# Eight DRAM-to-DRAM copies of kept cache rows, moved from the first feed-forward layer to the prompt's attention

## The chip, the cores and the metric

The kernel runs on one core of a Trainium2 chip. The metric is the device time of one execution, in microseconds. Before the change it is 1665.25 us (median of 3 runs, 1664.86 to 1665.97). TensorE (PE) multiplies, VectorE (DVE), ScalarE (ACT) and GpSimd (POOL) do elementwise work, and SyncE (SP) issues nearly all DMA transfers. Each engine works through its own list of instructions in the order in which it was built.

## The reference, cut to what matters

A two-layer decoder step on a 512-token prompt and 8 sampled sequences of 8 tokens. Layer 0 mixes by pooling, layer 1 by sparse attention; each layer is followed by a gated feed-forward network (FFN) with a causal convolution of width 3. All is float32.

```python
def conv_ffn(x, prefix, w_up, conv_w, conv_b, w_down):
    up = x @ w_up                       # 1024 -> 2 * 2816
    up_pad = jnp.concatenate([prefix, up], 1)
    c = conv_b
    for k in range(CONV_W):
        c = c + conv_w[k] * up_pad[:, k:k + T]
    g, u = jnp.split(c, 2, -1)
    return (jax.nn.silu(g) * u) @ w_down, up_pad[:, -(CONV_W - 1):]

def nsa_sample(...):
    ...
    buf_len = win_buf.shape[1]          # 512
    wkv = jnp.concatenate([win_buf, win_kv], 1)
    ...
    return o @ w_o, cmp_kv, slc_kv, wkv[:, -buf_len:]
```

The last value is the output `win_kv_s`: for each of the 8 sequences the 512 rows of its window, 8 of them new. The other 504 rows are those of the input `state_win_kv`, shifted by 8. They take part in no computation on the way to this output: they are copied from one place in DRAM to another, 1008 KB for each sequence.

## The kernel before

The activations of all 576 tokens stand in SBUF with the channels on the partitions, split into a high and a low part (`xh`, `xl`), so that three matmuls on rounded numbers make one precise product. A weight is split in the same way: SP fetches it into a raw buffer (`rawa`, two of them; line 235), ACT copies it to the rounded high part (`wha`, line 257), and DVE subtracts to get the low part (`wla`, line 258). Three pairs of high and low buffers take turns, so a split waits until PE is done with the pair three before it.

The FFN goes through its 2816 inner channels in units of 256. The unit that begins at chunk m0 of 128 channels has two weight blocks (gate and up). PE computes eight products for it, each of 24 matmuls of 288 columns (tiles `u`, line 166): for j in 0, 1 (which 128 channels), for each half of the tokens, for q in 0, 1 (gate, up). ACT then copies each product to SBUF (lines 419 to 421), starts the convolution (line 426), DVE finishes it (lines 427 and 428), ACT takes the silu (line 453), and DVE multiplies (line 454). After every second unit come the products of the down projection for the four chunks before (tiles `d`), with two weight blocks of their own, 192 matmuls in all. So the sequence of PE's work around the middle of layer 0 is: up 8, up 10, down of 4 to 7, up 12, up 14, down of 8 to 11, up 16, up 18, and so on, each of 192 matmuls.

In the program `keep_window(b)` (line 380) issues one of the eight copies, from SP. In layer 0 it is called behind the loads of the units m0 = 2 to 16, one copy for each.

The order of instructions on each engine is not the order of the code: a scheduler sets it when the program is built, by durations that it assumes for instructions and transfers. Moving a transfer in the code can therefore also move the instructions of other engines.

The prompt's attention comes much later, after the sampled tokens' attention. It works on 16 items (query head r of a group, pair p of key groups, branch j), four items for each r. An item's scores (`psp`, line 1534) go into two double banks of PSUM by turns, and DVE drains them (line 1539) into `P`; ACT takes exponentials (line 1540), POOL scales (line 1553), PE transposes (`ppp`) and multiplies with the values (`pop`, line 1582). `queries(r)` (line 1459) loads the queries of r from DRAM into `qs` with four DMAs (line 1462), `queries2(r)` transposes them on PE (`pq`) and copies them to `Q`. There are two buffers `qs`, so the load for r waits until the transposes of r - 2 are done. `plan` (line 1598) says at which item each of these steps is emitted: for r = 2 at item 4, for r = 3 at item 8.

Of the kernel before, what the change touches and what calls it, by code (L numbers as in the profile page):

```python
# [21 lines left out]
NB = 8  # L22
# [107 lines left out]
def body(tc, top, I, O):  # L130
    nc = tc.nc
# [28 lines left out]
    def f32(ap):  # L160
        return ap.bitcast(F32)
# [34 lines left out]
    def mmt(name, group="any", n=1):  # L196
        p_, size = banks[group]
        return p_.tile([128, 512] if n == 1 else [128, n, 512], F32, tag="ps" + group, name=name, bufs=size)
# [3 lines left out]
    def transpose(out, in_):  # L202
        pe.transpose(out, in_, ident[:in_.shape[0], :in_.shape[0]])
# [3 lines left out]
    def evac(out, in_):  # L207
        evac_turn[0] ^= 1
        if evac_turn[0]:
            act.activation(out, in_, AF.Copy)  # L210
        else:
            dve.tensor_copy(out, in_)
# [167 lines left out]
    def keep_window(b):  # L380
        rows = "(p j) k g c -> p (j k g c)"
        sp.dma_start(O["win_kv_s"][0, b, 0:WIN - TS].rearrange(rows, j=4), I["state_win_kv"][0, b, TS:WIN].rearrange(rows, j=4))

    def ffn(l, U, ctx, opening, closing, first=None):
# [22 lines left out]
        def products(blk, j, hf, name):  # L407
            p_ = mmt(name)
            terms = [(wt[:, k, j * 128:(j + 1) * 128], xt[:, k, hf * HALF:(hf + 1) * HALF])
                     for k in range(KD) for wt, xt in ((blk[0], xh), (blk[0], xl), (blk[1], xh))]  # L410
            mm3(p_[:, :HALF], terms)
            return p_

        def conv(m, pa, pb):
            u = fp.tile([128, UW + 8], F32, tag="u", name=f"u{l}{m}", bufs=4)
            us = u[:, 2 + TP:UW].rearrange("p (b t) -> p b t", t=2 + TS)
            pool.memset(u[:, 0:2], 0.0)
            pool.tensor_copy(us[:, :, 0:2], sTv[:, :, m].rearrange("p (b k) -> p b k", k=2))
            act.activation(u[:, 2:2 + HALF], pa[:, :HALF], AF.Copy)
            act.activation(u[:, 2 + HALF:2 + TP], pb[:, :TP - HALF], AF.Copy)  # L420
            act.activation(us[:, :, 2:], pb[:, TP - HALF:HALF].rearrange("p (b t) -> p b t", t=TS), AF.Copy)  # L421
            pool.tensor_copy(col[:, :, m].rearrange("p (j i) -> p j i", i=2),  # L422
                             u[:, TP:TP + 90].rearrange("p (j i) -> p j i", i=10)[:, :, 0:2])
            cf = fp.tile([128, UW], F32, tag="c", name=f"c{l}{m}", bufs=4)
            c = cf[:, 0:CW]
            act.activation(c, u[:, 2:UW], AF.Identity, bias=cv[:, 132 + m:133 + m], scale=cv[:, 88 + m:89 + m])  # L426
            dve.scalar_tensor_tensor(c, u[:, 1:1 + CW], cv[:, 44 + m:45 + m], c, OP.mult, OP.add)  # L427
            dve.scalar_tensor_tensor(c, u[:, 0:CW], cv[:, m:m + 1], c, OP.mult, OP.add)
            return cf

        def up(chunks):
            for c0 in range(0, len(chunks), 2):
                m0 = chunks[c0]
                wv = I["ffn_w_up"][l].rearrange("(k p) n -> p k n", p=128)
                if m0 == 0 and first:
                    wg, wu = first
                else:
                    wg = U.load(wv[:, :, m0 * 128:(m0 + 2) * 128])
                    wu = U.load(wv[:, :, FF + m0 * 128:FF + (m0 + 2) * 128])
                if l == 0 and 2 <= m0 < 2 + 2 * NB:  # L440
                    keep_window(m0 // 2 - 1)
                order = [(j, hf, q) for hf in range(2) for j in range(2) for q in range(2)] if m0 == 0 else \
                        [(j, hf, q) for j in range(2) for hf in range(2) for q in range(2)]
                pr = {}
                for n, (j, hf, q) in enumerate(order):
                    pr[j, hf, q] = products((wg, wu)[q], j, hf, f"u{l}{m0}{j}{hf}{q}")
                    if m0 == 0:
                        opening(n)
                for j in range(2):
                    m = m0 + j  # L450
                    cg = conv(m, pr[j, 0, 0], pr[j, 1, 0])
                    cu = conv(NF + m, pr[j, 0, 1], pr[j, 1, 1])
                    act.activation(cg[:, 0:CW], cg[:, 0:CW], AF.Silu)
                    dve.tensor_tensor(cu[:, 0:CW], cg[:, 0:CW], cu[:, 0:CW], OP.mult)
                    hh = fp.tile([128, T], F32R, tag="hh", name=f"hh{l}{m}", bufs=8)
                    hl = fp.tile([128, T], F32R, tag="hl", name=f"hl{l}{m}", bufs=8)

                    def views(full):
                        return (full[:, 0:TP], full[:, TP:].rearrange("p (b t) -> p b t", t=TS))

                    cs = (cu[:, 0:TP], cu[:, 2 + TP:2 + TP + 80].rearrange("p (b t) -> p b t", t=10)[:, :, 0:TS])
                    for hv, lv, s in zip(views(hh), views(hl), cs):
                        act.activation(hv, s, AF.Copy)
                        dve.tensor_tensor(lv, s, f32(hv), OP.subtract)
                    hp[m] = (hh, hl)
# [22 lines left out]
        def down(chunks, first, last):  # L488
# [11 lines left out]
            for m, hf in ([(m, hf) for hf in range(2) for m in range(KD)] if last else [(m, hf) for m in range(KD) for hf in range(2)]):  # L500
# [10 lines left out]
                if last:  # L511
                    closing(hf, m)
                    if hf == 0 and m in (3, 5):
                        state_out(m // 4)

        up(list(range(0, 4)))
        for g in range(1, 5):
            up(list(range(4 * g, 4 * g + 4)))
            down(list(range(4 * g - 4, 4 * g)), g == 1, False)
        up([20, 21])  # L520
        down(list(range(16, 22)), False, True)

# [873 lines left out]
    def prompt_attention(ctx):  # L1396
# [62 lines left out]
        def queries(r):  # L1459
            qs = qp.tile([128, 4, 256], F32, tag="qs", name=f"qs{r}")  # L1460
            for t in range(4):
                sp.dma_start(qs[:, t].rearrange("p (g c) -> p g c", g=4),
                             qd[t * 128:(t + 1) * 128].rearrange("p (g r c) -> r p g c", g=4, r=4)[r])
            gate[r] = gpv[:, :, :, r]
            return qs

        def queries2(r, qs):
            Q[r] = pa.tile([128, 2, TP], F32, tag="QT", name=f"Q{r}")
            for p in range(2):
                pt = tpt(f"pq{r}{p}")  # L1470
                for t in range(4):
                    transpose(pt[:, t * 128:(t + 1) * 128], qs[:, t, p * 128:(p + 1) * 128])
                evac(Q[r][:, p], pt)

        def cmp_scores(r):
            pk = mmt(f"pk{r}")
            for g in range(4):
                pe.matmul(pk[32 * g:32 * g + 32], KB[:, g], Q[r][:, g // 2], start=True, stop=True, tile_position=(0, 32 * g))
            ks = pp.tile([128, TP], F32, tag="ks", name=f"ks{r}", bufs=1)
            act.activation(ks, pk, AF.Copy, scale=-1.0)  # L1480
            return ks
# [24 lines left out]
        def cmp_probs(r, ec):  # L1506
            pt = tpt(f"pct{r}")
            for t in range(4):
                transpose(pt[:, t * 128:(t + 1) * 128], ec[:, t].rearrange("p g n -> p (g n)"))
            cmpp[r] = ptp.tile([128, TP], F32, tag="pc", name=f"pc{r}")  # L1510
            evac(cmpp[r], pt)
# [81 lines left out]
        for t in range(4):  # L1593
            keys(t)
            if t == 0:
                queries2(0, q0)
        pend = {}
        plan = {0: lambda r: pend.update(q=queries(r)), 1: lambda r: queries2(r, pend["q"]), 2: lambda r: pend.update(k=cmp_scores(r)),
                3: lambda r: pend.update(e=cmp_softmax(r, pend["k"])), 4: lambda r: cmp_probs(r, pend["e"])}
        n = len(items)  # L1600
        for i in range(n + 3):
# [11 lines left out]
            for r in range(1, 4):  # L1613
                k = i - 4 * (r - 1)
# [83 lines left out]
    with ExitStack() as ck:  # L1698
        with ExitStack() as cl:
# [10 lines left out]
            def opening(i):  # L1710
                norm[i][1].run(tile_steps(0))
                return during_first_half(norm[i][1])
# [107 lines left out]
        with ExitStack() as c1:  # L1820
            prompt_attention(c1)
# [41 lines left out]
```

## Time and profile before

| what | value |
|---|---|
| median of 3 runs | 1665.25 us |
| the profiled execution's own time | 1669.55 us |
| its span, first to last instruction | 1667.7 us |
| mean granted TensorE clock | 0.978 |
| PE busy | 1588.7 us, 95% |
| DVE, ACT, POOL busy | 61%, 45%, 23% |
| the eight copies | issued by SP from 44.3 to 256.4 us, 1008 KB each |

A profiled execution is one run on the chip, with the start and end of each instruction. All rows below are from it, and its own time is some 4 us over the median. Times in the rows are microseconds from the start of the span. An instruction's idle time is how long its engine stood still just before it, and the releaser is the instruction that ended the wait.

### The profile page before, as it was taken

What the parts mean: (1) busy time and instruction counts of PE and PEld (TensorE: products, weight loads), DVE (VectorE), ACT (ScalarE), POOL (GpSimd) and SP (SyncE); (2) the same over time, 40 slices, a digit from 0 to 9 for tenths busy, and PEclk for the clock granted to TensorE, in tenths of its full rate; (3) what the DMA queues carried; (4) which work ended last, traced back from release to release, by engine and by line L of the source; (5) the groups of instructions that cost most, each with busy time, mean ns of one, the idle gap of its engine ahead of it and who ended that gap; (6) DMA issues with size and microseconds to landing.
All of it is one profiled execution on the core that took longest, in us unless ns stands there. A gap on an engine that the chain in (4) does not pass through costs nothing.

```text
span 1667.7 us, 32288 instructions
## 1 busy us (share of the span) xinstructions
PE 1588.7 (95%) x13207; PEld 1485.2 (89%) x13207; DVE 1013.6 (61%) x2053; ACT 758.5 (45%) x1406; POOL 391.1 (23%) x597
## 2 busy tenths in 40 slices
PE   7999979899999999999999988999999999999995
PEld 7999979899999999999996764556999999999995
DVE  7665344454557435898878967675465645454547
ACT  5655141434335332466565665655255534334332
POOL 3222000011102001343333316662122201111104
PEclk9999988999999999999999998999999999999997
DMA  5334223222224684664549960004212223232211
GB/s 194 110 129 149 76 75 126 77 83 70 102 65 171 211 235 130 185 242 159 179 166 377 415 165 4 1 1 129 84 33 95 77 77 102 77 101 77 78 60 57
DMA packets 122323, 206.06 MB, mean 124 GB/s; under 512 B 18543, under 2 KB 98505, under 8 KB 112592
## 3 DMA queue, kind: packets, MB, share of 16 engines
q1 hardware_dynamic: 112272, 134.49, 25.4%
q0 software_dynamic: 9216, 67.11, 10.8%
q10 hardware_dynamic: 688, 2.40, 0.5%
q8 instruction: 104, 1.70, 0.4%
q14 instruction: 43, 0.35, 0.1%
HBM read 187.10 MB, written 24.84 MB: 127 GB/s over the span
## 4 chain that ended last, share of the span: by engine, by line
PE 78%; DVE 9%; issue 4%; POOL 4%; ACT 3%; DMA 2%; SPq 0%; ACTq 0%; POOLq 0%; DVEq 0%
PE u L166 32%; PE d L166 14%; PE pr L921 11%; PE pj L166 7%; PE wo L166 2%; POOL P L1553 2%; PE psp L1534 2%; DVE wla L258 1%; PE pop L1582 1%; PE po L1336 1%; DVE kf L1213 1%; PE pj L716 1%; DMA sr<-in_cache_slc_kv,idx 1%; PE pss L1241 1%; ACT P L1540 1%
## 5 line engine op out<-in xcount | busy, mean ns | idle before, releaser
L166 PE MATMUL u<-xh,wha 128*128 128x288 f32 x704 | 210.5, 299 | 7.9 <-ACT wha L257 7.9
L166 PE MATMUL u<-xh,wla 128*128 128x288 f32 x704 | 210.4, 299 | 7.6 <-DVE wla L258 7.6
L166 PE MATMUL u<-xl,wha 128*128 128x288 f32 x704 | 210.7, 299 | 0.3 <-POOL xl L352 0.2
L166 PE MATMUL u<-xl,whb 128*128 128x288 f32 x704 | 208.0, 296 | 0.2
L166 PE MATMUL u<-xh,whb 128*128 128x288 f32 x704 | 207.3, 295 | 0.0
L166 PE MATMUL u<-xh,wlb 128*128 128x288 f32 x704 | 207.2, 295 | 0.0
L422 POOL COPY fcol<-u 128x18 f32<-128x18 f32 x88 | 62.8, 726 | 506.4 <-ACT u L421 506.4
L427 DVE SCALAR_TENSOR_TENSOR c<-u,convp,c 128x592 f32<-128x592 f32 x88 | 71.9, 831 | 160.6 <-ACT c L426 160.6
L166 PEld LDWEIGHTS u<-xh,wla 128*128 128x128 f32 x704 | 134.6, 191 | 8.8 <-DVE wla L258 8.8
L166 PEld LDWEIGHTS u<-xh,wha 128*128 128x128 f32 x704 | 134.7, 191 | 8.4 <-ACT wha L257 8.4
L258 DVE TENSOR_TENSOR wlb<-rawb,whb 128x2048 fp32r<-128x2048 f32 x37 | 84.8, 2292 | 87.8 <-ACT whb L257 87.8
L166 PEld LDWEIGHTS u<-xl,wha 128*128 128x128 f32 x704 | 134.7, 191 | 2.0 <-DVE xl L352 1.1
L166 PEld LDWEIGHTS u<-xl,whb 128*128 128x128 f32 x704 | 132.0, 188 | 1.9 <-DVE xl L352 1.1
L258 DVE TENSOR_TENSOR wla<-rawa,wha 128x2048 fp32r<-128x2048 f32 (+1 forms) x52 | 99.3, 1917 | 54.2 <-ACT wha L257 54.2
L166 PEld LDWEIGHTS u<-xh,whb 128*128 128x128 f32 x704 | 132.0, 188 | 0.1
L166 PEld LDWEIGHTS u<-xh,wlb 128*128 128x128 f32 x704 | 132.0, 188 | 0.0
L510 DVE SCALAR_TENSOR_TENSOR xz<-xz,d 128x288 f32<-128x288 f32 x160 | 70.4, 450 | 97.4 <-PE d L166 96.8
L257 ACT ACTIVATE whb<-rawb 128x2048 fp32r<-128x2048 f32 x37 | 70.8, 1914 | 115.2 <-DMA rawb<-in_ffn_w_up 32.3
L257 ACT ACTIVATE wha<-rawa 128x2048 fp32r<-128x2048 f32 (+1 forms) x52 | 82.8, 1611 | 71.4 <-PE d L166 39.5
L166 PE MATMUL d<-hh,wha 128*128 128x288 f32 x352 | 105.5, 301 | 4.1 <-ACT wha L257 4.0
L921 PE MATMUL pr<-xlo,W1h 128*128 128x256 f32 x512 | 103.9, 285 | 2.5 <-DVE xlo L896 2.5
L894 ACT ACTIVATE xhi<-xf 128x1024 fp32r<-128x1024 f32 (+1 forms) x68 | 70.1, 1031 | 77.6 <-PE pr L921 55.6
(662 smaller groups left out, 4532.6 us busy)
## 6 DMA issues: line engine op xcount, KB each, us to landing
rawa<-in_ffn_w_up SPq DMA_DIRECT2D x22, 1024.0 KB
rawb<-in_ffn_w_up SPq DMA_DIRECT2D x22, 1024.0 KB
rawa<-in_ffn_w_down SPq DMA_DIRECT2D x11, 1024.0 KB
rawb<-in_ffn_w_down SPq DMA_DIRECT2D x11, 1024.0 KB
rawa<-in_nsa_w_in SPq DMA_DIRECT2D x9, 1024.0 KB
sr<-in_state_win_kv SPq DMA_DIRECT2D x8, 1024.0 KB
out_win_kv_s<-in_state_win_kv SPq DMA_DIRECT2D x8, 1008.0 KB
rawb<-in_nsa_w_o SPq DMA_DIRECT2D x16, 256.0 KB
```

The lines of the kernel that those rows point to most:

```text
L166: pe.matmul(out, a, b, start=first and j == 0, stop=last and j == n - 1)
L257: act.activation(h[:, a:b], r[:, a:b], AF.Copy)
L258: dve.tensor_tensor(lo[:, a:b], r[:, a:b], f32(h[:, a:b]), OP.subtract)
L422: pool.tensor_copy(col[:, :, m].rearrange("p (j i) -> p j i", i=2), u[:, TP:TP + 90].rearrange("p (j i) -> p j i", i=10)[:, :, 0:2])
L427: dve.scalar_tensor_tensor(c, u[:, 1:1 + CW], cv[:, 44 + m:45 + m], c, OP.mult, OP.add)
L510: dve.scalar_tensor_tensor(z, z, ALPHA if first else 1.0, p_[:, :HALF], OP.mult, OP.add)
L716: pe.matmul(*args, start=k == 0 and i == 0, stop=k == KD - 1 and i == 1)
L894: act.activation(xhi.rearrange(flat), xf.rearrange(flat), AF.Copy)
L921: pe.matmul(banks[b, kv][ri][:, :, gh * nn:(gh + 1) * nn], W1[wi][:, kv, ri * 8 + th * 4 + c], xx[:, c // 2, c % 2].rearrange("p g n -> p ...
L1213: dve.transpose(kv["k", n][:, :, :, at].rearrange("p f g (j n) -> p j g f n", j=4), raw[:, :, 0:256].rearrange("p j (g f i) -> p j g f i", ...
L1534: pe.matmul(views[e, t], Q[r][rs, p, t * 128:(t + 1) * 128], KT[rs, j, p, 0:n], start=True, stop=True)
L1553: pool.tensor_tensor(x, x, st[:, 2, e, t:t + 1].broadcast_to([128, (t + 1) * 128]), OP.mult)
```

## The change

The call in the FFN is removed. The copies are issued in the prompt's attention instead: four behind the query loads of r = 2, and four behind those of r = 3, with an order (`issue_after`) that keeps them behind the last of the four loads on SP's list. The copies themselves are the same eight.

```diff
@@ in ffn, up
-                if l == 0 and 2 <= m0 < 2 + 2 * NB:
-                    keep_window(m0 // 2 - 1)
@@ in prompt_attention
         pend = {}
-        plan = {0: lambda r: pend.update(q=queries(r)), 1: lambda r: queries2(r, pend["q"]), 2: lambda r: pend.update(k=cmp_scores(r)),
+
+        def next_queries(r):
+            pend["q"] = queries(r)
+            if r > 1:
+
+                with tc.issue_after(nc.cur_bb.bb.instructions[-1]):
+                    for b in range(NB // 2):
+                        keep_window(NB // 2 * (r - 2) + b)
+
+        plan = {0: next_queries, 1: lambda r: queries2(r, pend["q"]), 2: lambda r: pend.update(k=cmp_scores(r)),
```

The built lists differ in three places. Line numbers of the changed kernel from 440 on are 2 lower than those before, and from the end of `plan` on 7 higher.

The first place is layer 0's FFN. On ACT before, around the last products of unit 8; `u08110` is the product of layer 0, m0 = 8, j = 1, second half, q = 0; `wha15` and `wha16` are the two weight blocks of unit 10:

```order
L419 ACTIVATE u031_2589<-u08101_2473 128x288
L420 ACTIVATE u09_2578<-u08110_2498 128x224
L421 ACTIVATE u09_2578<-u08110_2498 128x8x8
L426 ACTIVATE c09_2585<-u09_2578,convp0_61 128x592
L453 ACTIVATE c09_2585<-c09_2585 128x592
L420 ACTIVATE u031_2589<-u08111_2523 128x224
L421 ACTIVATE u031_2589<-u08111_2523 128x8x8
L426 ACTIVATE c031_2596<-u031_2589,convp0_61 128x592
L257 ACTIVATE wha15_2610<-rawa15_2608 128x2048
L463 ACTIVATE hh09_2602<-c031_2596 128x512
L463 ACTIVATE hh09_2602<-c031_2596 128x64
L257 ACTIVATE wha16_2616<-rawa16_2614 128x2048
```

And the same stretch of ACT now:

```order
L419 ACTIVATE u031_2585<-u08101_2469 128x288
L257 ACTIVATE wha16_2612<-rawa16_2610 128x2048
L420 ACTIVATE u09_2574<-u08110_2494 128x224
L421 ACTIVATE u09_2574<-u08110_2494 128x8x8
L426 ACTIVATE c09_2581<-u09_2574,convp0_61 128x592
L257 ACTIVATE wha17_2878<-rawa17_2876 128x2048
L420 ACTIVATE u031_2585<-u08111_2519 128x224
L421 ACTIVATE u031_2585<-u08111_2519 128x8x8
L426 ACTIVATE c031_2592<-u031_2585,convp0_61 128x592
```

Both splits of unit 10's weights stood behind the convolution of unit 8's last products. Now `wha15` stands ahead of unit 8's first products (not shown), `wha16` ahead of the last two, and the first split of the work that follows (`wha17`) comes before the last one. DVE's subtractions (line 258) moved with them. The same happened at the other boundaries between units up to the down projection of chunks 8 to 11; PE's list there keeps its order but for the `d` matmuls of chunks 4 to 7.

The second place is SP's list at the prompt's attention, before (`fst` is the state that layer 1's FFN reads, `rawb` the weights of the attention's output projection and then the last norm's parameters):

```order
L1462 DMA qs_12645<-qd 128x4x64 x4
L1462 DMA qs_13048<-qd 128x4x64 x4
L392 DMA fst_14535<-in_state_ffn 128x5x128
L393 DMA fst_14535<-in_state_ffn 64x128
L1626 DMA rawb_13933<-in_nsa_w_o 64x4x256 x4
L1626 DMA rawb_14102<-in_nsa_w_o 64x4x256 x4
L1663 DMA rawb_14521<-in_ln_g 96x1024
L1664 DMA rawb_14521<-in_ln_b 96x1024
```

And now:

```order
L1460 DMA qs_12637<-qd 128x4x64 x4
L382 DMA out_win_kv_s<-in_state_win_kv 16x16128 x4
L1460 DMA qs_13044<-qd 128x4x64 x4
L382 DMA out_win_kv_s<-in_state_win_kv 16x16128 x4
L1633 DMA rawb_13933<-in_nsa_w_o 64x4x256 x4
L1633 DMA rawb_14102<-in_nsa_w_o 64x4x256 x4
L1670 DMA rawb_14521<-in_ln_g 96x1024
L1671 DMA rawb_14521<-in_ln_b 96x1024
L392 DMA fst_14535<-in_state_ffn 128x5x128
L393 DMA fst_14535<-in_state_ffn 64x128
```

Four copies stand between the query loads of r = 2 and r = 3, four behind those, and the load of `fst` moved behind the norm's parameters.

The third place is PE's list where the queries of r = 3 are transposed (`pq30`, `pq31`; `psp103` are the scores of item 10, tokens 384 to 511, and `ppp71a` a transpose of item 7's probabilities). Before:

```order
L203 MATMUL pq30_13141<-cst_58,qs3_13048 128x128 x4
L203 MATMUL pq31_13147<-cst_58,qs3_13048 128x128 x4
L203 MATMUL ppp71a_13153<-cst_58,P71_12867 128x128 x4
L203 MATMUL ppp71b_13160<-cst_58,P71_12867 128x128 x4
L203 MATMUL ppp71c_13167<-cst_58,P71_12867 128x128 x2
L1534 MATMUL psp103_13175<-KT_12097,Q2_12737 128x512 x2
L1534 MATMUL psp102_13178<-KT_12097,Q2_12737 128x384 x2
```

And now, from the same place on:

```order
L1532 MATMUL psp103_13175<-KT_12089,Q2_12733 128x512 x2
L1532 MATMUL psp102_13178<-KT_12089,Q2_12733 128x384 x2
L1532 MATMUL psp102_13178<-KT_12089,Q2_12733 128x128 x2
L1532 MATMUL psp101_13214<-KT_12089,Q2_12733 128x256 x2
L1580 MATMUL pop6_13131<-ppha70_13100,kvt0_12072 64x512
L1532 MATMUL psp113_13272<-KT_12089,Q2_12733 128x512 x2
L1532 MATMUL psp112_13275<-KT_12089,Q2_12733 128x384 x2
L1532 MATMUL psp112_13275<-KT_12089,Q2_12733 128x128 x2
L203 MATMUL pq30_13141<-cst_58,qs3_13044 128x128
L203 MATMUL pq31_13147<-cst_58,qs3_13044 128x128
L203 MATMUL ppp71a_13153<-cst_58,P71_12863 128x128
```

The scores of item 10 and most of item 11 stand ahead of the query transposes and of item 7's probabilities; the lists of DVE and ACT changed in the same stretch, POOL's did not. A few matmuls of the output projection (`wo`) and two additions on DVE beside the split of its weights also changed places.

## Rows read from the trace of the kernel before

**Rows 1.** Page: span, engines' busy time, granted PE clock in 40 slices.
```profile
span 1667.7 us, 32288 instructions
PE 1588.7 (95%) x13207; PEld 1485.2 (89%) x13207; DVE 1013.6 (61%) x2053; ACT 758.5 (45%) x1406; POOL 391.1 (23%) x597
PEclk9999988999999999999999998999999999999997
```

**Rows 2.** Windows: length, each engine's busy us (count), PE clock, DMA share, GB/s.
```profile
60.00:180.00 120.00, 119.67 (x899) 117.98 (x898) 67.61 (x102) 62.10 (x108) 26.37 (x52) 1.00 0.30 105
180.00:345.00 165.00, 144.59 (x1009) 142.38 (x1009) 70.51 (x83) 56.77 (x94) 11.86 (x43) 0.92 0.26 90
345.00:465.00 120.00, 120.00 (x908) 120.00 (x907) 61.37 (x82) 42.61 (x71) 16.73 (x31) 1.00 0.27 88
```

**Rows 3.** PE's waits, 40 to 560 us: total us, times, longest us.
```profile
PE u L166 <- ACT wha L257: 7.9, 2, 4.0
PE u L166 <- DVE wla L258: 7.6, 4, 2.5
PE d L166 <- ACT wha L257: 4.0, 1, 4.0
PE d L166 <- DVE wla L258: 0.9, 1, 0.9
```

**Rows 4.** PE's timeline at the first of these waits: start, us, instruction, idle before.
```profile
185.66 0.40 PE L166 MATMUL u<-xh,wla 128*128 128x288 f32 x1 [0.90 <-DVE wla L258]
```

**Rows 5.** Chain that ended last: start, us, engine, tile, line, count.
```profile
343.17 25.49 PE d L166 x192
```

**Rows 6.** ACT's timeline at the end of unit 8.
```profile
208.51 0.88 ACT L426 ACTIVATE c<-u,convp 128x592 f32<-128x592 f32 x1
213.11 1.89 ACT L257 ACTIVATE wha<-rawa 128x2048 fp32r<-128x2048 f32 x1
216.47 1.89 ACT L257 ACTIVATE wha<-rawa 128x2048 fp32r<-128x2048 f32 x1
```

**Rows 7.** Windows: loads with a copy, without one, and quiet.
```profile
184.00:200.00 16.00, 15.10 (x114) 14.87 (x113) 5.84 (x5) 3.62 (x9) 0.68 (x4) 1.00 0.56 197
280.00:296.00 16.00, 13.60 (x92) 13.60 (x93) 5.64 (x5) 2.18 (x5) 0.22 (x1) 0.89 0.40 132
196.00:200.00 4.00, 4.00 (x32) 4.00 (x32) 1.67 (x2) 2.05 (x5) 0.46 (x3) 1.00 0.00 0
```

**Rows 8.** ACT's timeline at the end of unit 16.
```profile
390.80 1.92 ACT L257 ACTIVATE wha<-rawa 128x2048 fp32r<-128x2048 f32 x1 [2.60 <-PE u L166]
394.00 1.92 ACT L257 ACTIVATE wha<-rawa 128x2048 fp32r<-128x2048 f32 x1
```

**Rows 9.** SP's timeline at the prompt's attention.
```profile
978.93 20.74 SPq L1462 DMA_DIRECT2D qs<-qd  x10
1138.75 0.39 SPq L392 DMA_DIRECT2D fst<-in_state_ffn  x1
1162.12 0.43 SPq L1664 DMA_DIRECT2D rawb<-in_ln_b  x1
```

**Rows 10.** First use of `fst`: PE, count, ns, first and last start.
```profile
L203 PE MATMUL fsp<-cst,fst x6: 272/272/273, 1214.3 to 1214.9; 128*128 128x128 f32 x5, 64*128 64x64 f32 x1
```

**Rows 11.** PE's timeline in the prompt's attention.
```profile
1080.79 1.09 PE L203 MATMUL pq<-cst,qs 128*128 128x128 f32 x8
...
1083.04 2.00 PE L1534 MATMUL psp<-KT,Q 64*128 64x512 f32 x12
...
1110.33 0.66 PE L203 MATMUL pct<-cst,ec 128*128 128x128 f32 x4 [2.48 <-POOL ec L1503]
```

**Rows 12.** DVE's drains of one item: ns min/median/max, first and last start.
```profile
L1539 DVE CUSTOM_DVE_ANT_0 P<-psp,cst x8: 286/486/692, 1084.2 to 1088.1; 128x512 f32<-128x512 f32 x2, 128x384 f32<-128x384 f32 x2, 128x128 f32<-128x128 f32 x2, 128x256 f32<-128x256 f32 x2
```

**Rows 13.** Windows in the prompt's attention.
```profile
1070.00:1080.00 10.00, 9.19 (x43) 5.34 (x43) 6.58 (x22) 6.79 (x23) 5.70 (x9) 0.66 0.00 0
1080.00:1090.00 10.00, 10.00 (x75) 6.03 (x71) 6.50 (x23) 6.11 (x21) 5.69 (x9) 1.00 0.01 2
```

## Prediction

> **What bounds the kernel now.** I read the page first. PE is busy for 95% of the span, and its granted clock is at or near full almost everywhere, with a dip in slices 5 to 8 of 40 and another in the middle [rows 1]. So time can be had where PE stands still, or runs at half clock after it stood still. Slices 5 to 8 are layer 0's FFN, the place that the change takes copies from. Next I cut that FFN into windows. From 60 to 180 us and from 345 to 465 us PE is busy throughout at clock 1.00; between them, from 180 to 345 us, it is busy for 144.59 of 165 us at a mean clock of 0.92 [rows 2]. The third view, PE's waits, names what was late: nearly only the splits of the weights on ACT and DVE, in eight waits of together 7.9 + 7.6 + 4.0 + 0.9 = 20.4 us [rows 3]. No wait on a DMA is among them.
>
> Why were the splits late? At the end of unit 8 ACT starts a convolution at 208.51, and only at 213.11 and 216.47 the two splits of the next unit's weights [rows 6]. The loads of these weights lie in the stretch from 184 to 200 us, and from 196 us on no transfer was running [rows 7]. So the weights had lain in SBUF for 17 us when ACT split them. ACT was idle or busy with other things, and the splits stood behind the convolution on its list, which itself waits for PE's last products. It is the built order that stalls PE, not the transfer.
>
> **The change part by part.** *The order in the FFN.* The change takes eight transfers out of the list that the scheduler plans with, and the splits move ahead: in the order rows of ACT, one block of unit 10 stands ahead of unit 8's convolutions altogether, and the other ahead of the last products. What this gives can be worked out from the total. The first of the eight waits ends at 185.66 and is 0.90 us long, so the stretch begins at 184.76 [rows 4]; it ends where the down projection of chunks 8 to 11 begins, at 343.17 [rows 5]. That is 158.4 us. In it lie five pieces of 192 matmuls (up 8, up 10, down, up 12, up 14), and one such piece without waits at full clock takes 25.49 us [rows 5], so 127.45 us would do. The loss is 158.4 - 127.45 = 31.0 us: 20.4 us of standing still [rows 3] and the other 10.6 us of half clock behind it.
>
> Does the new order wait for nothing? The kernel before already shows that order one boundary later. At the end of unit 16, ACT waits for PE to release a buffer, splits the block at 390.80, copies the product and starts its convolution, and splits the next block at 394.00 [rows 8]; PE is busy for all of the 120 us around it [rows 2]. The list now has that pattern at each boundary from 180 us on. What is late next is PE itself, so I take the whole 31.0 us. As lower bound I let one wait of 4.0 us [rows 3] stay, with its share of half clock (10.6 / 20.4 of it, 2 us): 25 us.
>
> *The copies in the FFN.* A stretch of 16 us with two loads and a copy has the DMA engines busy for 0.56 x 16 = 9.0 us, one with two loads alone for 0.40 x 16 = 6.4 us [rows 7]. So a copy costs about 2.6 us of all DMA engines. Taking it away shortens loads that nobody waits for: 0 us. Were that cover gone it would be 2.6 us for each pair of loads.
>
> The Trainium skill ("DMA: Bandwidth & Descriptors", section "Issuing engines are not separate DMA queues") states that all transfers run on the same 16 DMA engines and interleave. By that rule a copy delays the loads beside it, and a slow copy would be the cause of the waits. The quiet window before the late splits [rows 7] speaks against it; by the rule alone the change would take away no more than what I price as the second rival.
>
> *The copies in the attention.* SP issues the last ten query loads, those of r = 2 and r = 3 among them, from 978.93 to 999.7 us [rows 9]. Now four copies stand between those two sets, and four behind. Four take 4 x 2.6 = 10.4 us, so the queries of r = 3 land by about 1015 us at the latest. PE transposes them at 1080.79 [rows 11]. That leaves over 60 us, and the DMA engines are otherwise idle there [rows 13]: 0 us. Behind the copies on SP come the output projection's weights and then `fst`, which moved. SP held `fst` until 1138.75 before, and the transfers behind it went out up to 1162.12 [rows 9]; with `fst` behind those, it is issued at some 1163 us and first used at 1214.3 [rows 10]: 0 us. The `wo` matmuls that changed places cost nothing that I can see, since PE works on there without a gap that counts.
>
> *The order in the attention.* Here the scheduler takes the queries of r = 3 for late, and puts the scores of item 10 and three quarters of item 11 in front of their transposes. PE's work is the same, but the scores need PSUM that DVE must first drain. Twelve score matmuls take PE 2.0 us [rows 11]; the eight drains of one item take DVE from 1084.2 to about 1088.4 us, 4.2 us [rows 12]. PE, with two double banks, can be one double bank ahead of DVE. Before it writes the last of item 11's scores, DVE has to have drained item 10, some 5 us after the start, while PE has about 2.0 + 0.6 + 0.5 + 1 = 4.1 us to do until then. So PE stands still for about 1 us, in short pieces, and the transposes behind (for the values and the queries) come later by as much. This stretch is not bound by PE alone: at 1110.33 PE waits 2.48 us for POOL [rows 11]. I take +1.5 us. The lower end is -2.5 us, if the new order makes that wait go away. For the upper end I take another wait of that size and a clock drop like that of the window from 1070 us, which at 0.66 loses 3.4 us of 10 [rows 13]: +5.9 us.
>
> The Trainium skill ("TensorE: Matmul & The Clock Gate", section "HAM oscillation — how this bites in real kernels") says that waits between bursts of matmuls put the clock back to half, and that each such change is paid for again. It speaks against this change in the attention. The trace agrees: the clock is 0.66 behind waits there [rows 13]. By the rule the upper end would be the value, 4.4 us more than the sum.
>
> *Sum.* Against the profiled execution: 1669.55 - 31.0 + 1.5 = 1640.0 us, with a span of 1667.7 - 29.5 = 1638.2 us [rows 1]. That execution lies 4.3 us above the median, so the median goes from 1665.25 to 1635.75: **1636 us**.
>
> **The rivals.** *First, the second splits stay late.* The first split of each pair goes ahead, but PE still waits for DVE's subtractions. They are 7.6 + 0.9 = 8.5 us [rows 3], with their share of half clock 12.9 us, so 18.1 us are gained: 1665.25 - 18.1 + 1.5 = 1649 us. For it: DVE's list is the fuller one. Against it: at the end of unit 16 the same lists left PE no wait [rows 2, 8].
>
> *Second, the order does nothing*, and only transfers beside each other cost. Then the FFN gains 0, since no transfer ran when PE waited [rows 7], and the attention costs its 1.5 us: 1667 us.
>
> *Third, slower: the queries of r = 3 arrive late.* They stand behind four copies on the same queue. If a copy from DRAM to DRAM alone ran on one DMA engine in place of 16, it would take 16 x 2.6 = 42 us, four of them 166 us, and the queries issued near 1000 us would land at about 1155 us, 75 us behind their use at 1080.79 [rows 9, 11]: 1665.25 - 31 + 75 = 1709 us. It begins to cost when a copy takes over 20 us, and makes the kernel slower than before from 28 us on. Against it: in the FFN all 16 engines together account for the copy at 2.6 us [rows 7].
>
> *Within the forecast*, the attention can cost its upper end: 1640 us.
>
> **How the numbers follow.** The forecast gets 0.87, with a range of its own from 1665.25 - 31.0 - 2.5 = 1631.8 to 1665.25 - 25 + 5.9 = 1646.2 us; the first rival 0.07, the second 0.03, the third 0.03. A range from 1631 to 1646 us leaves out the rivals and a little of the forecast's ends. A measurement of this kernel can tell some 0.2% (3.3 us) from no change. Faster is the forecast and the first rival: 0.94; the second rival is the same: 0.03; the third is slower: 0.03.
>
> **What would show it.** Right: PE has no wait on `wha` or `wla` from 159 us on until the last down projection, its clock is 1.00 there, and layer 0's FFN ends 31 us earlier; the second block's split on ACT comes ahead of the copies of the last products, about 3 us before the unit's end. In the attention the copies fill the DMA engines for about 10 us at a time, nobody waits for `qs`, and the stretch from the first scores to the output projection is between 2.5 us shorter and 6 us longer. Wrong: waits of 2 to 4 us at the same boundaries with only another name (first rival), ACT held by a split while a product waits to be copied, or PE waiting for the `pq` transposes.

## The result, and the profile after

The changed kernel takes 1636.62 us (median of 4 runs, 1633.42 to 1638.4); the kernel before, beside it, 1665.07 us (4 runs, 1664.86 to 1665.97). The ratio is 0.9826, with a 95% interval from 0.9809 to 0.9843. The forecast was 1636 us. That it hit so closely is luck in part: its sum has two errors that nearly cancel, and the experiments below say which.

The profiled execution of the changed kernel took 1636.72 us. From its page: span, busy time of PE, and PE's granted clock in 40 slices.

```profile
span 1634.9 us, 32308 instructions
PE 1575.9 (96%) x13207; PEld 1476.0 (90%) x13207; DVE 1013.6 (62%) x2053; ACT 757.3 (46%) x1406; POOL 405.9 (25%) x597
PEclk9999999999999999999999999999999999999997
```

The dip in slices 5 to 8 [rows 1] is gone. The windows of layer 0's FFN answer to [rows 2]; the columns are length, then PE, PEld, DVE, ACT and POOL busy (count), clock, DMA share, GB/s:

```profile
60.00:180.00 120.00, 119.67 (x899) 117.98 (x898) 72.45 (x104) 61.57 (x108) 28.91 (x52) 1.00 0.27 87
180.00:345.00 165.00, 165.00 (x1247) 165.00 (x1247) 82.74 (x105) 63.63 (x103) 26.39 (x48) 1.00 0.26 82
345.00:465.00 120.00, 119.88 (x906) 119.61 (x905) 60.86 (x90) 44.11 (x75) 16.57 (x29) 1.00 0.25 79
```

From 180 to 345 us PE is now busy for 165.00 us (144.59 before) at clock 1.00 (0.92 before). Its waits from 40 to 560 us (total us, times, longest) answer to [rows 3]; none is on a weight split any more:

```profile
PE pm L166 <- ACT xh L595: 0.7, 1, 0.7
PE pj L166 <- POOL xl L352: 0.2, 1, 0.2
PE u L166 <- POOL xl L352: 0.2, 1, 0.2
PE lnt L203 <- DVE xz L605: 0.2, 1, 0.2
```

ACT's timeline at a unit's end shows why (before: [rows 6]). A split of the next weights now starts ahead of the copy of the last product (L420) and of the convolution (L426):

```profile
206.77 1.92 ACT L257 ACTIVATE wha<-rawa 128x2048 fp32r<-128x2048 f32 x1 [2.60 <-PE u L166]
208.59 0.34 ACT L420 ACTIVATE u<-u 128x224 f32<-128x224 f32 x1
...
209.13 0.89 ACT L426 ACTIVATE c<-u,convp 128x592 f32<-128x592 f32 x1
209.97 1.92 ACT L257 ACTIVATE wha<-rawa 128x2048 fp32r<-128x2048 f32 x1
```

The matmuls of that FFN's last down products end the stage. Their row gives ns min/median/max and the first and last start in the window from 465 us on, of before:

```profile
L166 PE MATMUL d<-hh,wla x96: 293/296/298, 470.6 to 513.8; 128*128 128x288 f32 x96
```

and of after:

```profile
L166 PE MATMUL d<-hh,wla x37: 293/295/303, 464.9 to 482.5; 128*128 128x288 f32 x37
```

The stage ends 513.8 - 482.5 = 31.3 us earlier. The span is shorter by 1667.7 - 1634.9 = 32.8 us, so all the rest together gives 1.5 us. SP's timeline at the attention (before: [rows 9]), and the DMA share there (last two columns of the windows):

```profile
956.17 2.61 SPq L382 DMA_DIRECT2D out_win_kv_s<-in_state_win_kv  x4
966.43 3.10 SPq L1460 DMA_DIRECT2D qs<-qd  x4
969.58 4.87 SPq L382 DMA_DIRECT2D out_win_kv_s<-in_state_win_kv  x4
...
1138.55 0.39 SPq L392 DMA_DIRECT2D fst<-in_state_ffn  x1
```

```profile
960.00:970.00 10.00, 1.00 0.94 314
970.00:980.00 10.00, 0.83 1.11 361
980.00:990.00 10.00, 1.00 0.33 105
990.00:1000.00 10.00, 1.00 0.00 0
```

The copies run up to about 983 us, and nothing waits for `qs` or `fst`. Two places did change on PE. In round 3 of the attention (before: [rows 11]) there are two new short waits, and a shorter one at `pct`; in the output projection a wait for `wlb` is new:

```profile
1049.88 0.70 PE L1532 MATMUL psp<-KT,Q 64*128 64x256 f32 x4 [0.55 <-DVE st L1537]
1055.53 0.66 PE L203 MATMUL ppp71b<-cst,P 128*128 128x128 f32 x4 [0.57 <-DVE ppha L1566]
1078.47 0.66 PE L203 MATMUL pct<-cst,ec 128*128 128x128 f32 x4 [1.12 <-POOL ec L1501]
1137.66 0.40 PE L166 MATMUL wo<-xh,wlb 128*128 128x288 f32 x1 [1.56 <-DVE wlb L258]
```

DVE's timeline has the reason of the last one. The split `wlb` stands behind four additions to `xz`, each of which needs a finished product of PE; the last two rows of that stretch:

```profile
1134.94 0.45 DVE L1653 SCALAR_TENSOR_TENSOR xz<-xz,wo 128x288 f32<-128x288 f32 x1 [2.71 <-PE wo L166]
1135.32 2.28 DVE L258 TENSOR_TENSOR wlb<-rawb,whb 128x2048 fp32r<-128x2048 f32 x1
```

Before, the same split ran ahead of these additions:

```profile
1159.35 2.28 DVE L258 TENSOR_TENSOR wlb<-rawb,whb 128x2048 fp32r<-128x2048 f32 x1
```

### The profile page after: what moved, and what is told of

Its sections match the earlier page's. It is cut to its first block, busy times and chain, and to the rows that moved or that the text cites. A ratio compares the mean times of both kernels' runs of the same rounds, so it can differ in the third digit from the quotient of the medians.

```text
span 1634.9 us, 32308 instructions
## 1 busy us (share of the span) xinstructions
PE 1575.9 (96%) x13207; PEld 1476.0 (90%) x13207; DVE 1013.6 (62%) x2053; ACT 757.3 (46%) x1406; POOL 405.9 (25%) x597
## 5 line engine op out<-in xcount | busy, mean ns | idle before, releaser
L422 POOL COPY fcol<-u 128x18 f32<-128x18 f32 x88 | 68.4, 787 | 468.0 <-ACT u L421 468.0
L508 DVE SCALAR_TENSOR_TENSOR xz<-xz,d 128x288 f32<-128x288 f32 x160 | 70.1, 450 | 86.8 <-PE d L166 86.2
L919 PE MATMUL pr<-xhi,W1h 128*128 128x256 f32 x512 | 105.4, 288 | 0.0
```

The costliest lines, as they stand in the source:

```text
L508: dve.scalar_tensor_tensor(z, z, ALPHA if first else 1.0, p_[:, :HALF], OP.mult, OP.add)
L919: pe.matmul(banks[b, kv][ri][:, :, gh * nn:(gh + 1) * nn], W1[wi][:, kv, ri * 8 + th * 4 + c], xx[:, c // 2, c % 2].rearrange("p g n -> p ...
```

## The experiments

Theory: the built order of the splits cost the 31 us, and the copies' transfers cost nothing, in either place. Rival: the transfers beside the weight loads cost it. Three groups ran on three chips; the second and third are 0.7 to 0.8% slower for the kernel before, so medians are compared within a group only. In the first group the kernel before has 1662.43 us (15 runs), in the second 1674.23 (17), in the third 1675.93 (11).

**1. The old order without the copies.** Edges that only order ACT's list put 15 splits (`hi`) behind the instruction that stood ahead of each before (`seen` collects the instructions by kind).

```diff
+    EDGES = ((('hi', 4), ('c', 8)), (('hi', 5), ('ua', 11)), (('hi', 6), ('ua', 14)), ...
...
+        if l == 0:
+            for (ka, a), (kb, b) in EDGES:
+                tc.add_manual_dep(seen[ka][a].ins, seen[kb][b].ins.name, NOSYNC, reason="order")
```

> The changed kernel with the splits' old places put back: no copy runs in the first FFN, but ScalarE is made to issue the weight splits of units 6 to 14 and of the first two down blocks behind the same convolution instructions as in the kernel before (15 order-only edges; nothing waits for a result it did not wait for). TensorE's order in that stage is then the one of before. Theory (the order of the splits costs the time, not the transfers): TensorE waits again for wha and wla between 180 and 345 us, some 16 to 20 us, with half clock behind the waits, and the median goes back to 1667 us (1660 to 1670). Rival (the copies' traffic beside the weight loads costs the time): with no copy there the stage stays full, 1637 us (1633 to 1641).

Measured: 1659.5 us (11 runs, 1656.8 to 1663.62), ratio to before 0.9989 (0.9979 to 1.0). PE's waits from 180 to 345 us:

```profile
PE u L166 <- ACT wha L263: 7.9, 2, 4.0
PE u L166 <- DVE wla L264: 4.5, 2, 2.4
PE d L166 <- ACT wha L263: 4.0, 1, 4.0
PE d L166 <- DVE wla L264: 0.5, 1, 0.5
```

The three waits on ACT are back to the tenth of a microsecond [rows 3], with no copy anywhere near. The stage ends at 509.0 us, so 26.5 of 31.3 us come back with edges on ACT's list alone. DVE's subtractions follow ACT's copies: at the end of unit 8 they start at 215.55 and 218.51 us (215.67 and 218.63 before). The time is half a microsecond below the theory's range: two of DVE's waits are missing; no edge held DVE's list. Experiment 5 closes that.

**2. Most of the traffic with the new order.** Each copy is cut at row 384; the scheduler then builds ACT's list in the first FFN as in the changed kernel, though eight copies stand there again.

```diff
-        sp.dma_start(O["win_kv_s"][0, b, 0:WIN - TS]...
+        sp.dma_start(O["win_kv_s"][0, b, lo:hi]...
-                    keep_window(m0 // 2 - 1)
+                    keep_window(m0 // 2 - 1, 0, 384)
...
+            if r == 3:
+                with tc.issue_after(nc.cur_bb.bb.instructions[-1]):
+                    for b in range(NB):
+                        keep_window(b, 384, WIN - TS)
```

> The kernel before with 384 of each sequence's 504 kept rows copied in the first FFN as before (76% of the bytes, eight DMAs of 768 KB) and the other 120 rows copied behind the loads of queries(3); ScalarE's order in the first FFN is then that of the changed kernel, and attention and out-projection keep the order of before. The output is complete. Theory (order): the first FFN gives all of its 30.4 us though three quarters of the traffic stay, and neither the reorder in the attention (+1.5) nor that in the out-projection (+1.8) is there: 1665.1 - 30.4 = 1634.7, or less by the attention's clock, 1633 us (1630 to 1636), below the changed kernel. Rival (traffic): 76% of the loss stays, 1665.1 - 0.24 x 30.4 = 1658 us (1652 to 1662).

Measured: 1633.59 us (5 runs, 1632.17 to 1636.2), ratio 0.9836 (0.9822 to 0.985). The window that lost the time:

```profile
180.00:345.00 165.00, 165.00 (x1247) 165.00 (x1247) 84.98 (x106) 63.57 (x103) 26.43 (x48) 1.00 0.29 97
```

97 GB/s beside 82 in the changed kernel, and PE does not wait once; the stage ends at 482.7 us (changed kernel: 482.5). So three quarters of the traffic cost nothing there, and the rival falls; experiment 5 shows the other side, the loss without any copy. With eight copies of 1008 KB at these places the scheduler builds the old order, with eight of 768 KB the new one. The likely reason is that it counts a transfer by its length and puts a split where it takes the load to have landed; no run looked into the scheduler.

**3. No copies at all.** This is the kernel before without the call; it leaves the kept rows of the output unwritten.

```diff
-                if l == 0 and 2 <= m0 < 2 + 2 * NB:
-                    keep_window(m0 // 2 - 1)
```

> The kernel before without the eight copies (the kept rows of the sliding window's cache are not written). All engines but SP then run in the order that the split version has. Theory: what the copies' traffic costs anywhere is the difference to the split version, and it is within 1 us: 1633 us (1630 to 1636). Rival (traffic costs, in the first FFN or in the attention): 3 us or more below the split version.

Measured: 1634.3 us (5 runs, 1629.31 to 1641.31), ratio 0.9837 (0.9812 to 0.9863). It is 0.7 us above experiment 2 by the medians: the copies cost nothing that shows, within spreads of 4 and 12 us.

**4. All copies behind the queries of round 3.**

```diff
-            if r > 1:
+            if r == 3:
...
-                    for b in range(NB // 2):
-                        keep_window(NB // 2 * (r - 2) + b)
+                    for b in range(NB):
+                        keep_window(b)
```

> The changed kernel with all eight copies behind the loads of queries(3), none behind those of queries(2). The pq matmuls of the third round and what stands round them are then back in the order of before, the late split in the out-projection stays where the change put it. Theory (the +1.5 of the attention came from that reorder, the +1.8 of the out-projection from the late split): 1.5 us below the changed kernel, 1635 us (1632 to 1637), with TensorE waiting 1.6 us in the out-projection as in the changed kernel and about 2.5 us at the pct matmuls of round 3 as before. Rival (the +1.5 came from traffic of the first four copies beside the attention): eight copies in one place cost as much or more, 1637 to 1640 us.

Measured: 1634.89 us (5 runs, 1632.29 to 1635.84), ratio 0.9838 (0.9825 to 0.9852): inside the theory's range, but the median can't tell 1.5 us. The trace can: from round 2's `pct` matmuls to round 3's it takes 38.6 us (the table below has all kernels). It also says more than the theory. PE's wait at round 3's `pct` is that of before again:

```profile
1073.14 0.66 PE L203 MATMUL pct<-cst,ec 128*128 128x128 f32 x4 [2.48 <-POOL ec L1501]
```

and behind it the clock falls, as it did before (length, PE busy, clock, DMA share, GB/s; a window's clock is a mean of full speed, 1.00, and half, 0.50):

```profile
1073.00:1077.00 4.00, 3.82 (x17) 0.61 0.00 0
1077.00:1081.00 4.00, 4.00 (x30) 0.97 0.00 0
```

In the kernel before:

```profile
1110.00:1114.00 4.00, 3.19 (x16) 0.69 0.00 0
1114.00:1118.00 4.00, 4.00 (x18) 0.50 0.00 0
```

In the changed kernel, where the wait is 1.12 us, it stays at full speed:

```profile
1078.00:1082.00 4.00, 2.84 (x18) 1.00 0.00 0
1082.00:1086.00 4.00, 4.00 (x30) 1.00 0.00 0
```

The length of the wait does not decide this alone. At round 2's `pct` the profiles of all 13 runs here have the wait at 2.47 to 2.50 us, and half clock follows in six of them. At round 1's, ten have it at 2.48 or 2.49 us, and half clock follows in two. Round 2 in the changed kernel:

```profile
1035.89 0.66 PE L203 MATMUL pct<-cst,ec 128*128 128x128 f32 x4 [2.48 <-POOL ec L1501]
1036.00:1040.00 4.00, 3.47 (x18) 0.62 0.00 0
```

and in experiment 6:

```profile
1045.14 0.66 PE L203 MATMUL pct<-cst,ec 128*128 128x128 f32 x4 [2.49 <-POOL ec L1501]
1045.00:1049.00 4.00, 3.01 (x20) 1.00 0.00 0
```

**5. The old order on DVE too.** As experiment 1, with four more edges for DVE's splits (`lo`) and PE's groups of `u` products kept in their order.

```diff
+    EDGES = (... (('lo', 8), ('z', 14)), (('lo', 9), ('z', 15)), (('lo', 14), ('z', 31)), (('lo', 15), ('z', 31)))
...
-            pe.matmul(out, a, b, start=first and j == 0, stop=last and j == n - 1)
+            with tc.issue_after(before[-1]) if keep and before and not j else ExitStack():
+                pe.matmul(out, a, b, start=first and j == 0, stop=last and j == n - 1)
```

> As the late-split run, and with four splits of VectorE (wla of units 8 and 12 to 14) put back behind the additions of the down products as well, TensorE's groups kept in the order of before; still no copy in the first FFN. Theory (the 5 us that the late-split run did not give back are the waits of 0.90 and 2.48 us for wla that it lacked, and the half clock behind them): all eight waits of before are there, 20 us in all, and the first FFN ends where it ended before: 1662 to 1664 us on this chip, 3 to 5 us above the late-split run. Rival (those 5 us were the copies' traffic): the waits do not come back or cost nothing, 1659.5 us as in the late-split run.

It ran in the second group. Measured: 1675.15 us (12 runs, 1671.39 to 1683.81) beside 1674.23 us of before, ratio 1.0005 (0.9986 to 1.0024). The waits:

```profile
PE u L169 <- ACT wha L268: 7.9, 2, 4.0
PE u L169 <- DVE wla L269: 7.9, 4, 2.5
PE d L169 <- ACT wha L268: 3.9, 1, 3.9
```

19.7 of the 20.4 us are back, one wait of 0.9 us is not, and the stage ends at 511.8 us. Its numbers in us are those of another chip, but relative to before the gain is gone, with no copy in the stage. Order explains 511.8 - 482.5 = 29.3 of 31.3 us; the wait that is missing, with half clock behind it, can be the rest, but that was not shown.

**6 and 9. One split of the output projection put back.**

```diff
+            if u == 2:
+                split = nc.cur_bb.bb.instructions[-1]
...
-            half(u, 0)
+            with tc.issue_after(split):
+                half(u, 0)
```

> The changed kernel with one split of the out-projection put back ahead of the four additions that the change left it behind (one order-only edge; no other instruction of any engine moves). Theory: TensorE's wait of 1.6 us for wlb at the third unit goes, the time from the first wo matmul to layer 1's first matmul falls from 60.9 to 59.1 us, and the median is 1.8 us below the changed kernel run beside it. Rival (the wait only moves to the next unit's split, whose load lands late): 60.9 us stay, and no difference.

Measured: 1642.74 us (5 runs, 1641.62 to 1650.2), ratio 0.9828 (0.9799 to 0.9858), beside 1645.95 us for the changed kernel (experiment 8). PE's `wo` products (first and last start) in this kernel, and in the changed one:

```profile
L166 PE MATMUL wo<-xh,wlb x128: 290/295/382, 1128.4 to 1184.6; 128*128 128x288 f32 x128
```

```profile
L166 PE MATMUL wo<-xh,wlb x128: 290/294/398, 1121.8 to 1179.8; 128*128 128x288 f32 x128
```

They take 56.2 us instead of 58.0: the 1.8 us hang on this one instruction. In the median it did not show when repeated in the third group:

> The kernel with the one split put back, once more, since the chip of its first run spread over 8 us and more. Theory: in its segments it is the sum of the best found: first FFN without waits, round 3's pct wait at 1.1 us with full clock behind it, 59.1 us in the out-projection, so 1.8 us below the changed kernel beside it. Rival: the segment is won and given back at a later boundary; then the median is that of the changed kernel.

Measured: 1646.92 us (5 runs, 1644.07 to 1648.28), ratio 0.9824 (0.9801 to 0.9847). The segment was 59.1 us again, as expected; the median equals that of the changed kernel beside it (1646.95). Whether this version beats the changed kernel as a whole stays open.

**7. Each copy twice.**

```diff
                         keep_window(NB // 2 * (r - 2) + b)
+                        keep_window(NB // 2 * (r - 2) + b)
```

> The changed kernel with each of the eight copies issued twice (16 DMAs of 1008 KB, the second of each pair writing the same rows again); the instructions of all engines but SP keep their order. Theory (the copies stand where nothing waits for a transfer): same as the changed kernel within 1 us. Rival (they use up room that the loads behind them need): eight more times 2.6 to 3 us of all DMA engines, 21 to 24 us, push the loads behind them and TensorE waits for wo or the split of its raw rows: 5 us or more above the changed kernel.

Measured: 1648.48 us (5 runs, 1644.64 to 1652.66), ratio 0.9833 (0.9807 to 0.9859): 2.5 us above the changed kernel by the median, which neither theory named and which lies within both spreads; by their ratios they are 0.0008 apart. The profiled spans are equal (1650.9 and 1650.6 us). SP's timeline:

```profile
970.21 25.23 SPq L382 DMA_DIRECT2D out_win_kv_s<-in_state_win_kv  x8
995.49 3.29 SPq L1460 DMA_DIRECT2D qs<-qd  x4
```

Eight copies kept SP's queue for 25.23 us, 3.2 us each, and the queries of round 3 went out at 995.49, 13.4 us later than in the changed kernel on the same chip (982.08). PE still did not wait for them.

**8, 10 and 11. The changed kernel and experiment 2 again.**

> The changed kernel itself beside the others, on their chip. By its ratio of 0.9826 to the kernel before it is 1633.5 us here, where the kernel before has 1662.4 us. It is also a second profile of the same program: if the half clock behind the wait at round 3's pct matmuls belongs to the order of instructions, it is absent here too; if it belongs to the single execution, it may be there.

Measured: 1645.95 us (5 runs, 1642.25 to 1652.38), ratio 0.9825 (0.9798 to 0.9853). The ratio came out as expected, the absolute time did not: the kernel before is slower on this chip too. The half clock behind round 3's `pct` matmuls is absent again.

> The split version (384 rows copied in the first FFN, 120 in the attention) beside the same two. By the segments of the profiles it has 59.1 us in the out-projection (1.8 us less than the changed kernel) and, from round 2's pct matmuls to the first wo matmul, the kernel before's 82.4 to 86.8 us in place of the changed kernel's 83.0 to 85.5 us: 0.5 us below the changed kernel on the mean, 1.3 us above the kernel with the one split put back.

Measured: 1645.99 us (6 runs, 1641.59 to 1651.45), ratio 0.9834 (0.9811 to 0.9857). No difference among the three can be told.

> The changed kernel beside the two, and a third profile of it: 60.9 us from the first wo matmul to layer 1's first matmul, 42.9 us from round 3's pct matmuls to the first wo matmul, no wait in the first FFN.

Measured: 1646.95 us (5 runs, 1646.46 to 1648.99), ratio 0.9835 (0.9813 to 0.9858). All three segments came out as expected.

## Why the prediction came out right

Start times from PE's timeline of each profile, in us: the first FFN's end (last start of `d`), then the stretches from round 2's `pct` matmuls to round 3's, from there to the first `wo` matmul, and from there to layer 1's first `u`.

| kernel | FFN ends | pct 2 to 3 | pct 3 to wo | wo to u |
|---|---|---|---|---|
| before | 513.8 | 41.1 | 45.67 | 59.1 |
| 2 split; again (10) | 482.7; 482.6 | 38.6; 38.6 | 45.60; 43.71 | 59.1; 59.1 |
| 3 none | 484.5 | 41.1 | 45.64 | 59.1 |
| 4 all behind round 3 | 482.7 | 38.6 | 43.83 | 61.0 |
| changed; again (8); again (11) | 482.5; 483.0; 483.3 | 42.6; 42.6; 42.8 | 42.94; 42.94; 42.94 | 60.9; 61.0; 61.0 |
| 7 double | 482.6 | 40.0 | 42.95 | 60.9 |
| 1 late | 509.0 | 40.0 | 42.94 | 61.0 |
| 5 late, both | 511.8 | 40.0 | 42.94 | 61.0 |
| 6 one split back; again (9) | 483.0; 483.6 | 40.0; 42.6 | 42.94; 42.94 | 59.2; 59.1 |

**The FFN, -31.0: right, in size and in cause.** Measured -31.3. The stage of 158.4 us that should take 127.45 [rows 4, 5] now holds no wait and takes 311.71 - 184.46 = 127.25 us. That the wait was one on the order, read from the quiet window [rows 7], is what experiments 1, 2 and 5 show. The first two rivals fall with it. Some 0.9 us are given back before the attention: the third `pkp` product there starts at 954.44 instead of 984.88, 30.4 us earlier.

**The copies, 0 in both places: right, as far as the runs can tell.** PE does not wait for `qs` or `fst`, and copying twice left the profiled span as it was; a cost under the spread of the medians is not ruled out. Their price was a little low: 2.6 us of all DMA engines, against 25.23 / 8 = 3.2 us of SP's queue in experiment 7, with a DMA share of 0.90 meanwhile. The third rival needed 20 us for one copy.

**The order in the attention, +1.5: right up to `pct`, wrong from there on.** Up to round 3's `pct` matmuls the mechanism and the price were right: 40.0 instead of 38.6 us, or 42.6 to 42.8 instead of 41.1 where half clock follows round 2's wait, which comes and goes with the execution: +1.4 to +1.7. What failed is that the step stopped there. The later arrival at `pct` takes PE's wait for POOL from 2.48 to 1.12 us, and the half clock that followed it in all five profiles with the old order follows in none of the eight with the new. That gives back 0.8 to 2.7 us: from `pct` to the first `wo` matmul it is 42.94 or 42.95 us in the eight, 43.71 to 45.67 in the five. In the two first profiles the net is 85.5 - 86.8 = -1.3 us; among profiles that agree on the half clock at round 2 it lies between -1.3 and +0.6. So it is near nothing, not +1.5. That it is the shorter wait that saves the clock fits the 13 profiles, but was not shown: the same wait at rounds 1 and 2 is not always followed by half clock, and the order ahead of round 3's `pct` changed too. The prediction had this wait in its lower bound, -2.5, "if the new order makes that wait go away", and put its value elsewhere. The Trainium skill ("TensorE: Matmul & The Clock Gate", section "HAM oscillation — how this bites in real kernels") says of matmuls with waits between their bursts that the clock falls back in each wait and that the cost is paid each time. The traces agree in part: behind this wait it fell in five of five profiles at round 3, and in six of 13 at round 2. The upper end of +5.9, which by that rule would have been the value, did not come: the two new short waits, of 0.55 and 0.57 us, had no half clock behind them.

**The output projection, "cost nothing that I can see": wrong, +1.8.** The order rows showed that two additions on DVE and a split of weights had changed places; in the trace the split stands behind four. I took the price from PE's rows of before alone, where there was no gap. The gap was made by the change: the split now starts at 1135.32, behind four additions that each need a product of PE, and PE stands still for it from 1136.1 on. Experiments 6 and 9 show that it is this one instruction.

**The sum.** Between the two profiled executions: -31.3 in the FFN, +0.9 behind it, -2.9 from `pkp` to round 1's `pct`, -1.3 in round 3, +1.8 in the output projection, together -32.8. The -2.9 can't be put down to the change: that stretch took 46.1 us before and 43.2 after, but 45.0 and 41.8 in two more profiles of the changed kernel, and 47.8 in experiment 7. It may be one reason why the profiled execution of before was 4.3 us above its median. Without it -29.9 remain, beside a forecast of -29.5 and a measured median difference of -28.5. That the FFN's 31 us came is not luck. That the sum hit to within a microsecond is: the +1.8 that it lacked and the +1.5 that did not come are nearly the same.

## What to carry to other kernels

Where a scheduler orders the program, a transfer can cost time without delaying another one: it changes the order that is built, and with it the place of the work that reads other loads. If PE waits for work on data that landed long ago, compare the lists, not the queues. And when a change reorders a list, price every place that moved, on the engine that feeds PE too, and follow each up to the next wait: a later arrival can shorten that wait and give the time back.

## What was not expected of the hardware

- At round 3's `pct` a wait of 2.48 us was followed by half clock in each of five profiles (worth 0.8 to 2.7 us), one of 1.12 or 1.13 us in none of eight. At round 2's the wait was 2.47 to 2.50 us in all 13, and half clock followed in six: three of three with the changed kernel, one of two with experiment 6's.
- In the second group the changed kernel took 1645.95 instead of 1636.62 us. The first FFN ended alike (483.0 and 482.5 us); the third `pkp` product came 13.8 us later (968.28 and 954.44), behind a stage that keeps the DMA engines busy (from 850 to 940 us 361 GB/s here, 378 there). In that window the ten profiles without weight waits in the first FFN have 378 to 382 GB/s in the runs of the result and the first group, 359 to 365 in the second and third. So it seems to go with the chip; why is open.
- SP's queue issued eight copies of 1008 KB in 25.23 us: the loads behind them on that queue go out only then.
